# The preparation of an RWKV-7 layer in one written TensorE order, its key norms with tokens on partitions

## The chip, the cores and the metric

One core of one Trainium2 chip runs the whole kernel: two decoder layers over 256 tokens of width 2048, all in float32. The metric is the device time of one execution in microseconds, as the median of the runs.

## The reference, cut to what matters

The change lies in the even layer, in what comes ahead of its recurrence (group A) and of its window attention (group B):

```python
h = x @ e_w_in                                  # 256 x 2048 times 2048 x 4640
# A: 16 heads of 64; r, k, v of 1024 columns each, then low ranks of 64, 64 and 160
h = h + (token_shift(h) - h) * mu
w = -softplus(-(w0 + tanh(lw) @ w_up)) - 0.5;  decay = exp(-exp(w))
a = sigmoid(a0 + la @ a_up);  g = sigmoid(lg) @ g_up
kk = heads(k * k_k);  kk = kk / max(sqrt(sum(kk * kk, -1)), 1e-12)
k = k * (1 + (a - 1) * k_a)
# a scan over the tokens, for each head a state S of 64 x 64
S = S * decay + (S @ -kk) (kk * a)^T + v k^T;   y = S @ r
y = (y - mean(y)) * rsqrt(var(y) + 64e-5) * gn_w + gn_b + sum(r * k * r_k) * v
ya = y * g
# B: q of 1024, k and v of 128 columns: rotary, softmax over 128 tokens with sinks
mix = concat(ya, yb) @ e_w_out
```

After it come a layer norm, a SwiGLU, a second norm and a gated embedding, then the odd layer with the same.

## The kernel before, in words

**Products.** A float32 matrix is split into a rounded part `hi` and a rest `lo`, and a product is three TensorE products, `hi` by `xh`, `lo` by `xh`, `hi` by `xl`. Weights come in pieces of 2 x 128 rows: SyncE loads `raw`, ScalarE (ACT) casts `hi` (L151), VectorE (DVE) subtracts `lo` (L152); `hi` and `lo` have three buffers each, `raw` four. `gemm_steps` (L178 to L180) makes tokens by 512 columns in 96 products of 512 columns; `gemm_t` (L201, L203, L205) makes features by tokens, 192 products of 256 columns for 512 features. Small float32 products stand between them.

**The even layer's preparation**, `wkv_operands`, follows one path for two halves of 512 features (c = 0, 1):
- `incoming` loads x; for each of eight pairs j of 128 columns TensorE turns x (L216, four transposes), and ACT and DVE split it into `xh` and `xl` (L222, L223). The first `gemm_t` makes the low ranks out of it, 18 products for each j.
- From the low ranks come decays and gates (L586, L590, L591) and rates `a` (L625).
- `gemm_t` for k; the squares of kk are summed over a head's 64 features with the selector `sel` as weights (L633: 8 x 256 out), and the inverse norm is made on 8 partitions (two reciprocals and a square root with one Newton step). `gemm_t` for r.
- For each 128 features f: the norm is spread back (L651), decays are cumulated (L660), and DVE and ACT make the operands `ar` and `bk`. For each two f: the 32 x 32 blocks of the system to be solved (L689), copied into `blk` (L693).
- `values(0)` makes v for 512 columns, its token shift by DMA (`vs`, L719 to L721) and a copy with the head's mean removed (L723 to L725).
- The inverse of all 32 x 32 blocks, on DVE: a masked copy (L730), a transpose (L732), 30 steps of two operations (L739, L741), two transposes (L745, L746) into `Tc` and `TTc`.

Then `swa_project` makes keys (256 columns) and the first 512 columns of queries of group B, with rotary and transposes (L928, L945).

**The recurrence**, `wkv_chunks`, runs in units of 4 heads and 128 tokens. A unit makes masked matrices `lmat` (products L789, copies L790), solves with `Tc`, `TTc` (from L800 on) and ends in a tail on DVE (L880 to L891). `weave` runs two units at a time with products from a side: `values(1)` beside the first two units, the second 512 columns of queries beside the next two, the output projection and attention beside the rest.

**What sets the order.** In `wkv_operands` and for the first part of `swa_project` a scheduler orders every engine's instructions. From the first `weave` on TensorE's order is the written one. Each engine works its queue from the front: an instruction that waits holds up what stands behind it.

Of the kernel before, what the change touches and what calls it, by code (L numbers as in the profile page):

```python
# [18 lines left out]
P = 128  # L19
# [61 lines left out]

def take(steps, n):

    for _ in range(n):
        if next(steps, 0) == 0:
            return
        yield


class Trunk:  # L90
# [16 lines left out]
    def psum(self, mm, sm, sx=0):  # L107

        ctx = ExitStack()
        pool = lambda n, b: ctx.enter_context(self.tc.tile_pool(name=n, bufs=b, space=PSUM, reuse_waits="tile"))  # L110
        self.mm, self.sm = pool("mm", mm), pool("sm", sm)
        self.sx = pool("sx", sx) if sx else self.sm
        return ctx
# [70 lines left out]
    def gemm_t(self, lhs, view, n0, widths):  # L184
# [7 lines left out]
        for j, (xh, xl) in enumerate(lhs):  # L192
            hi, lo = next(ws)
            for kk in range(2):
                k = 2 * j + kk
                f0 = 0
                for i, w in enumerate(widths):
# [8 lines left out]
                                     skip_group_check=True)  # L206
        return [acc[i // 2][:w, i % 2] for i, w in enumerate(widths)]
# [203 lines left out]
def even_layer(T, a, src):  # L411
# [4 lines left out]
    with ExitStack() as ctx:  # L416
        ev = ctx.enter_context(tc.tile_pool(name="ev", bufs=1, reuse_waits="tile"))
        with tc.tile_pool(name="prep", bufs=1) as pr, T.psum(4, 4):
            ops, xT, values = wkv_operands(T, src, w_in, a, ev, pr)
            y = ops[-2]  # L420
        with tc.tile_pool(name="pairs", bufs=2, reuse_waits="tile") as pp, T.psum(2, 4, 2):
# [6 lines left out]
            swa = swa_project(T, pp, xT, w_in, a)  # L428
            qkv = next(swa)
            while next(swa) is None:  # L430
                pass
# [26 lines left out]
            with tc.manual_schedule(engines={mybir.EngineType.PE}):  # L458
                side = values(1, pp)
# [11 lines left out]
                side = zip_links(turned(), attend(range(4)), 2)  # L471
# [18 lines left out]
def wkv_operands(T, src, w_in, a, ev, pr):  # L490
    tc, nc = T.tc, T.nc
    xT = []
# [24 lines left out]
    nc.sync.dma_start(out=vec[50:51, 0:32], in_=mu[3328:3360].rearrange("(n p) -> n p", p=32))  # L517
    vps = T.sm.tile([P, 64], F32, name="s")
# [11 lines left out]
    early = tc.tile_pool(name="early", bufs=1)  # L530
    er = early.__enter__()
    gup0 = er.tile([P, AW], F32, name="gup0")
    gup1 = er.tile([32, AW], F32, name="gup1")
    nc.sync.dma_start(out=gup0, in_=a["e_g_up"][0][0:128])
    nc.sync.dma_start(out=gup1, in_=a["e_g_up"][0][128:160])
# [23 lines left out]
    for i in range(2):  # L559
        nc.vector.tensor_tensor(out=cum[:, i], in0=cum[:, i], in1=half, op=ALU.subtract)  # L560
# [8 lines left out]
    lg0 = er.tile([P, SEQ], F32, name="lg0")  # L569
    lg1 = er.tile([32, SEQ], F32, name="lg1")  # L570
    mix(ps[0], P, MU_L, lm)
    mix(ps[1], P, MU_L + 1, lg0)
    mix(ps[2], 32, MU_L + 2, lg1)
    nc.scalar.activation(out=lm[0:64], in_=lm[0:64], func=AF.Tanh)
    nc.scalar.activation(out=lg0, in_=lg0, func=AF.Sigmoid)
    nc.scalar.activation(out=lg1, in_=lg1, func=AF.Sigmoid)
# [3 lines left out]
    for c in range(2):  # L580
        cs = slice(c * 512, (c + 1) * 512)
        w0 = T.row(a["e_w0"][0], c * 512, 512, "brow", pr, 2)
        for t in range(NT):
            ts = slice(t * P, (t + 1) * P)
            z = T.sm.tile([P, 512], F32, name="s")
            nc.tensor.matmul(z, lm[0:64, ts], ups[0:64, cs], start=True, stop=True)  # L586
            nc.vector.tensor_tensor(out=sig[t][:, cs], in0=z, in1=w0, op=ALU.add)
            nc.scalar.activation(out=sig[t][:, cs], in_=sig[t][:, cs], func=AF.Sigmoid)
            g = T.sm.tile([P, 512], F32, name="s")
            nc.tensor.matmul(g, lg0[:, ts], gup0[:, cs], start=True, stop=False)  # L590
            nc.tensor.matmul(g, lg1[:, ts], gup1[:, cs], start=False, stop=True)  # L591
            nc.scalar.copy(out=gate[t][:, cs], in_=g)
    early.__exit__(None, None, None)
    T.rotary_tables(a["positions"][0])


    late = tc.tile_pool(name="late", bufs=1, reuse_waits="tile")
    lt = late.__enter__()
# [6 lines left out]
    for b in range(4):  # L605
        nc.vector.tensor_copy(out=m32[32 * b:32 * b + 32], in_=mtri[32 * b:32 * b + 32, 32 * b:32 * b + 32])
# [6 lines left out]
    ft = lambda n: lt.tile([P, SEQ], F32, name=n, bufs=4)  # L613
    bs = [ev.tile([P, AH], F32, name=f"bs{t}") for t in range(NT)]
    for c in range(2):
        k, kk, av, rks = [], [], [], []
        ps = T.gemm_t(xT, w_in, AW + c * 512, [128] * 4)
        for i in range(4):
            k.append(ft("k"))
            mix(ps[i], P, MU_K + 4 * c + i, k[i])  # L620
        ss = T.sm.tile([8, SEQ], F32, name="s")
        for i in range(4):
# [3 lines left out]
            av.append(ft("a"))  # L626
            nc.scalar.activation(out=av[i], in_=pa, func=AF.Sigmoid, bias=col[:, A0 + f:A0 + f + 1])
            kk.append(ft("kk"))
            nc.vector.tensor_scalar(out=kk[i], in0=k[i], scalar1=col[:, KK + f:KK + f + 1], scalar2=None,
                                    op0=ALU.mult)  # L630
            sq = lt.tile([P, SEQ], F32, name="sq")
            nc.scalar.activation(out=sq, in_=kk[i], func=AF.Square)
# [611 lines left out]
```

## Time and profile before

| | us |
|---|---|
| median of 3 runs | 2597.84 (2597.6 to 2606.3) |
| profiled execution | 2597.83 |
| its span, first to last instruction | 2595.9 |
| TensorE (PE) busy | 2541.7 (98%) |
| VectorE (DVE) busy | 1478.8 (57%) |
| ScalarE (ACT) busy | 1140.3 (44%) |
| even layer up to the end of the recurrence | about 475 |

Times in rows are microseconds from the span's start. A matmul's recorded time is longer than its share of the engine, since products overlap: the start of one to the start of the next is what it costs. Idle time stands in square brackets with what ended it.

### The profile page before, as it was taken

The numbers are of one execution on the slowest core, as the hardware profiler recorded it, in microseconds if no ns is written. First come the engines' busy times: TensorE is split into PE (matmuls) and PEld (weight loads), VectorE is DVE, ScalarE is ACT, GpSimd is POOL, SyncE is SP. The second block draws the span as 40 slices with busy tenths as digits, with TensorE's granted clock in tenths as the row PEclk, the third lists the DMA queues.
The fourth block names the chain that finished last, engine by engine and source line by source line (L and its number), as shares of the span: only waits on it lengthen the run. The fifth ranks groups of instructions, "written<-read, shape, count | busy, mean of one in ns | idle before, by whom it ended". The sixth has DMA issues, their size and how long they took to land.

```text
span 2595.9 us, 32573 instructions
## 1 busy us (share of the span) xinstructions
PE 2541.7 (98%) x12509; PEld 2083.3 (80%) x12509; DVE 1478.8 (57%) x2144; ACT 1140.3 (44%) x1508; POOL 60.3 (2%) x126
## 2 busy tenths in 40 slices
PE   8999989999999999999999999999999999999999
PEld 6887766778888888888888888887888888888877
DVE  4668556774544454455756666657454444445574
ACT  5563344444444344443444444435444334444343
POOL 0002110000000000000000000000000000000000
PEclk9999989999999999999999999999999999999999
DMA  6445322666666666666666555557666666666654
GB/s 190 129 119 170 106 66 74 199 208 190 187 190 191 194 197 187 189 189 192 201 193 193 170 171 168 165 171 220 193 187 188 193 194 194 187 189 188 193 179 159
DMA packets 240858, 458.56 MB, mean 177 GB/s; under 512 B 15345, under 2 KB 21155, under 8 KB 240703
## 3 DMA queue, kind: packets, MB, share of 16 engines
q1 hardware_dynamic: 240702, 456.48, 58.2%
q8 instruction: 98, 1.61, 0.2%
q14 instruction: 58, 0.47, 0.1%
HBM read 453.28 MB, written 2.10 MB: 175 GB/s over the span
## 4 chain that ended last, share of the span: by engine, by line
PE 90%; DVE 5%; ACT 1%; DMA 1%; issue 1%; POOL 0%; SPq 0%; DVEq 0%; ACTq 0%; POOLq 0%
PE acc L178 27%; PE acc L180 26%; PE acc L179 26%; PE acc L201 1%; PE acc L205 1%; PE acc L203 1%; DVE lo L152 1%; PE s L216 1%; DVE lmat L790 1%; ACT hi L151 0%; PE s L806 0%; PE s L1090 0%; PE s L1118 0%; DMA lnb<-in_ln_b_dram 0%; DMA raw<-in_e_w_in_dram 0%
## 5 line engine op out<-in xcount | busy, mean ns | idle before, releaser
L152 DVE TENSOR_TENSOR lo<-raw,hi 128x1024 fp32r<-128x1024 f32 (+1 forms) x840 | 1018.4, 1214 | 936.9 <-ACT hi L151 935.7
L151 ACT CAST hi<-raw 128x1024 fp32r<-128x1024 f32 (+1 forms) x840 | 875.3, 1043 | 1196.5 <-PE acc L180 1073.6
L178 PE MATMUL acc<-hi,x0h 128*128 128x512 f32 (+1 forms) x292 | 119.8, 410 | 1.8 <-ACT x L923 0.8
L180 PE MATMUL acc<-hi,x0l 128*128 128x512 f32 (+1 forms) x292 | 117.3, 402 | 0.0
L178 PE MATMUL acc<-hi,x1h 128*128 128x512 f32 (+1 forms) x292 | 116.6, 399 | 0.0
L179 PE MATMUL acc<-lo,x5h 128*128 128x512 f32 (+1 forms) x292 | 113.5, 389 | 2.1 <-DVE lo L152 2.1
L178 PE MATMUL acc<-hi,x6h 128*128 128x512 f32 (+1 forms) x292 | 114.4, 393 | 1.2 <-DVE x L288 1.2
L178 PE MATMUL acc<-hi,x2h 128*128 128x512 f32 (+1 forms) x292 | 115.5, 396 | 0.0
L178 PE MATMUL acc<-hi,x4h 128*128 128x512 f32 (+1 forms) x292 | 115.5, 396 | 0.0
L179 PE MATMUL acc<-lo,x0h 128*128 128x512 f32 (+1 forms) x292 | 115.4, 395 | 0.0
L178 PE MATMUL acc<-hi,x5h 128*128 128x512 f32 (+1 forms) x292 | 115.3, 395 | 0.0
L179 PE MATMUL acc<-lo,x3h 128*128 128x512 f32 (+1 forms) x292 | 113.7, 389 | 1.4 <-DVE lo L152 1.3
L178 PE MATMUL acc<-hi,x3h 128*128 128x512 f32 (+1 forms) x292 | 115.0, 394 | 0.0
L179 PE MATMUL acc<-lo,x4h 128*128 128x512 f32 (+1 forms) x292 | 113.6, 389 | 1.4 <-DVE lo L152 1.4
L179 PE MATMUL acc<-lo,x6h 128*128 128x512 f32 (+1 forms) x292 | 113.5, 389 | 1.4 <-DVE lo L152 1.4
L180 PE MATMUL acc<-hi,x1l 128*128 128x512 f32 (+1 forms) x292 | 114.6, 393 | 0.0
L179 PE MATMUL acc<-lo,x2h 128*128 128x512 f32 (+1 forms) x292 | 113.9, 390 | 0.4 <-DVE lo L152 0.4
L178 PE MATMUL acc<-hi,x7h 128*128 128x512 f32 (+1 forms) x292 | 114.0, 391 | 0.0
L179 PE MATMUL acc<-lo,x1h 128*128 128x512 f32 (+1 forms) x292 | 113.9, 390 | 0.0
L180 PE MATMUL acc<-hi,x2l 128*128 128x512 f32 (+1 forms) x292 | 113.9, 390 | 0.0
L180 PE MATMUL acc<-hi,x3l 128*128 128x512 f32 (+1 forms) x292 | 113.7, 390 | 0.0
L180 PE MATMUL acc<-hi,x4l 128*128 128x512 f32 (+1 forms) x292 | 113.5, 389 | 0.0
(571 smaller groups left out, 5082.3 us busy)
## 6 DMA issues: line engine op xcount, KB each, us to landing
raw<-in_ffn_w_dram SPq DMA_DIRECT2D x528, 512.0 KB, 3.6
raw<-in_o_w_in_dram SPq DMA_DIRECT2D x96, 512.0 KB, 3.8
raw<-in_e_w_in_dram SPq DMA_DIRECT2D x64, 512.0 KB, 3.7
raw<-in_ple_w_gate_dram SPq DMA_DIRECT2D x64, 512.0 KB, 4.8
raw<-in_e_w_out_dram SPq DMA_DIRECT2D x32, 512.0 KB, 4.9
raw<-in_o_w_out_dram SPq DMA_DIRECT2D x32, 512.0 KB, 4.0
x<-in_x_dram SPq DMA_DIRECT2D x16, 256.0 KB, 4.4
lng<-in_ln_g_dram SPq DMA_DIRECT2D x16, 256.0 KB, 3.3
```

The lines of the kernel that those rows point to most:

```text
L151: nc.scalar.copy(out=hi, in_=raw)
L152: nc.vector.tensor_tensor(out=lo, in0=raw, in1=hi.bitcast(F32), op=ALU.subtract)
L178: nc.tensor.matmul(o, xh[:, kk, s], hi[:, kk], start=k == 0, stop=False)
L179: nc.tensor.matmul(o, xh[:, kk, s], lo[:, kk], start=False, stop=False)
L180: nc.tensor.matmul(o, xl[:, kk, s], hi[:, kk], start=False, stop=k == 2 * n - 1)
L201: nc.tensor.matmul(o, hi[:, kk, fs], xh[:, kk], start=k == 0 and i % 2 == 0, stop=False, skip_group_check=True)
L203: nc.tensor.matmul(o, lo[:, kk, fs], xh[:, kk], start=False, stop=False, skip_group_check=True)
L205: nc.tensor.matmul(o, hi[:, kk, fs], xl[:, kk], start=False, stop=k == nk - 1, skip_group_check=True)
L216: nc.tensor.transpose(ps[:, kk, t * P:(t + 1) * P], src[t][:, kk * P:(kk + 1) * P], self.ident)
L790: nc.vector.copy_predicated(lm4[:, i].rearrange("p a b -> p (a b)"), mask, pl.rearrange("p a b c -> p (a b c)"))
```

## The change

`wkv_operands` gets a written order. For its first part (x, the low ranks) PE, ACT and DVE all keep the order in which the program issues, and `incoming` turns one j ahead of the product; from then on TensorE alone does. The small products are cut into steps, and `through` lets one step follow each step of a projection (12 products of 256 columns, or 6 of 512): decays and gates in the k projection of half 0, squares in r's, operands of half 0 in k's and r's of half 1, operands of half 1 in `values(0)` and the first queries, whose projection now stands ahead of the keys'. The inverse is issued beside the queries and keys. Transposes of queries and keys wait in a list `late` and are put at counted places of a later projection.

The norms' sums have tokens on partitions: the squares are the weights and `sel` with 8 columns is streamed (L686), one power on GpSimd makes the inverse norm, two transposes bring it back. The separate copy of v without its mean goes; the mean is taken from y (three DVE operations on `py` where ACT had a copy). Half of `cum` and the mask `m32` are made on GpSimd.

```diff
+def trailing(steps, late, at):
+    n = 0
+    while True:
+        try:
+            next(steps)
+        except StopIteration as e:
+            return e.value
+        yield
+        n += 1
+        if late and n in at:
+            late.pop(0)()
...
-        for j in range(8):
-            if j % 2 == 0:
+        for j in range(9):
+            if j < 8 and j % 2 == 0:
...
-            xT.append(T.split_t([x[t][:, j * 256:(j + 1) * 256] for t in range(NT)], f"x{j}", T.xt))
-            yield xT[-1]
-    ps = T.gemm_t(incoming(), w_in, 3 * AW, [128, 128, 32])
+            if j < 8:
+                xT.append(T.split_t([x[t][:, j * 256:(j + 1) * 256] for t in range(NT)], f"x{j}", T.xt))
+            if j:
+                yield xT[j - 1]
+    first = T.gemm_t_steps(incoming(), w_in, 3 * AW, [128, 128, 32])
+    manual = tc.manual_schedule(engines={E.PE, E.Activation, E.DVE})
+    manual.__enter__()
+    last(take(first, 10))
...
-            nc.tensor.matmul(ss, sel[:, i], sq, start=i == 0, stop=i == 3)
...
+                nc.tensor.matmul(ss[:, t], sq[i][:, t * P:(t + 1) * P], sel[:, i], start=i == 0 and t == 0,
+                                 stop=i == 3, skip_group_check=True)
+            yield
+        n = lt.tile([P, NT, 8], F32, name="norm")
+        nf = n.rearrange("p t h -> p (t h)")
+        nc.vector.tensor_scalar(out=n, in0=ss, scalar1=1e-24, scalar2=None, op0=ALU.max)
+        nc.gpsimd.tensor_tensor(out=nf, in0=nf, in1=T.mhalf, op=ALU.pow)
...
+        at = {0: (feature, 0), 4: (feature, 1), 9: (feature, 2), 11: (blocks, 2 * c, 0), 12: (blocks, 2 * c, 1),
+              13: (feature, 3), 20: (blocks, 2 * c + 1, 0), 21: (blocks, 2 * c + 1, 1), 22: (bonus, 0), 23: (bonus, 1)}
...
-            vm = pool.tile([P, 8], F32, name=f"vm{t}", bufs=1)
-            nc.vector.tensor_reduce(out=vm, in_=v3[t][:, h], axis=AX.X, op=ALU.add)
-            nc.vector.tensor_scalar(out=vm, in0=vm, scalar1=1.0 / HD, scalar2=None, op0=ALU.mult)
-            nc.vector.tensor_tensor(out=vs3[t][:, h], in0=v3[t][:, h],
-                                    in1=vm[:, :, None].to_broadcast([P, 8, HD]), op=ALU.subtract)
...
+    through(products(("k", 0), AW), side)
+    last(side)
+    with tc.tile_pool(name="late", bufs=1, reuse_waits="tile") as lt:
...
+        last(rates(0, lt))
+        through(products(("r", 0), 0), ks[0])
+        last(ks[0])
+        through(products(("k", 1), AW + 512), os[0])
+        through(products(("r", 1), 512), os[0], ks[1])
+        last(os[0])
+        last(ks[1])
+        through(values(0, pr), os[1])
+        swa = keys_, queries, late, qkv = swa_project(T, xT, w_in, a)
+        through(queries(0, pr), os[1], inv, inv)
+        through(trailing(keys_(), late, (9, 12)), os[1], inv)
+        last(inv)
...
-            nc.scalar.copy(out=y, in_=py)
+            nc.vector.tensor_reduce(out=var, in_=py, axis=AX.X, op=ALU.add)
+            nc.vector.tensor_scalar(out=var, in0=var, scalar1=1.0 / HD, scalar2=None, op0=ALU.mult)
+            nc.vector.tensor_tensor(out=y, in0=py, in1=var[:, :, None].to_broadcast([P, G, HD]), op=ALU.subtract)
...
-                side = swa
+                side = queries(1, pp)
...
-                side = zip_links(turned(), attend(range(4)), 2)
+                side = zip_links(trailing(turned(), late, (4, 7)), attend(range(4)), 2)
```

What stands in a row is shown at three places. **ACT at the start**, where `hi` is a cast of a weight piece and `x0h`, `x1h` and so on are casts of a turned j. Before:

```order
L151 CAST hi<-raw 128x576 x3
L222 CAST x0h<-s 128x512
L222 CAST x1h<-s 128x512
L151 CAST hi<-raw 128x576 x2
L222 CAST x2h<-s 128x512
L222 CAST x3h<-s 128x512
L222 CAST x4h<-s 128x512
L151 CAST hi<-raw 128x576 x3
```

ACT in the changed kernel, from its first cast:

```order
L237 CAST x0h<-s 128x512
L237 CAST x1h<-s 128x512
L165 CAST hi<-raw 128x576
L237 CAST x2h<-s 128x512
L165 CAST hi<-raw 128x576
L237 CAST x3h<-s 128x512
L165 CAST hi<-raw 128x576
```

The casts went from groups to turns: each `hi` but the first now stands behind the cast of the next j, and on TensorE the transposes of that j stand behind the 18 products of the j before last.

**DVE where the inverse begins**, whose first operation is the masked copy into `blk`. Before:

```order
L676 TENSOR_TENSOR kk<-r,k 128x256
L152 TENSOR_TENSOR lo<-raw,hi 128x1024
L698 COPY bs_539<-s 128x8
L698 COPY bs_540<-s 128x8
L152 TENSOR_TENSOR lo<-raw,hi 128x1024
L730 COPY_PREDICATED blk_536<-m_531,blk_538 128x1024
```

DVE in the changed kernel at the same operation (L798 there):

```order
L790 TENSOR_TENSOR vs_2057<-vs_2057,brow 128x512
L789 TENSOR_TENSOR vs_2058<-vs_2058,v_507 128x512
L791 TENSOR_TENSOR v_506<-vs_2057,v_506 128x512
L790 TENSOR_TENSOR vs_2058<-vs_2058,brow 128x512
L166 TENSOR_TENSOR lo<-raw,hi 128x1024
L791 TENSOR_TENSOR v_507<-vs_2058,v_507 128x512
L166 TENSOR_TENSOR lo<-raw,hi 128x1024
L798 COPY_PREDICATED blk_501<-m_496,blk_503 128x1024
```

The whole of `values(0)` moved ahead of the inverse: on TensorE the last blocks (L750 there) now stand after 132 products of 512 columns of v and queries, where 25 stood ahead of them.

**TensorE ahead of the first solve product**, which reads the inverse `blk` and `lmat`. Before:

```order
L789 MATMUL s<-ar_1176,bk_1177 128x256 x2
L945 MATMUL sx<-ident,q 128x128 x4
L789 MATMUL s<-ar_1176,bk_1177 128x256 x2
L789 MATMUL s<-ar_1203,bk_1204 128x256
L945 MATMUL sx<-ident,q 128x128 x4
L789 MATMUL s<-ar_1203,bk_1204 128x256 x3
L178 MATMUL acc<-hi,x0h 128x512
L800 MATMUL s<-blk_538,lmat_2226 32x32 x8
```

TensorE in the changed kernel at the same place:

```order
L883 MATMUL s<-ar_1316,bk_1317 128x256 x4
L883 MATMUL s<-ar_1419,bk_1420 128x256 x4
L192 MATMUL acc<-hi,x0h 128x512
L193 MATMUL acc<-lo,x0h 128x512
L194 MATMUL acc<-hi,x0l 128x512
L894 MATMUL s<-blk_503,lmat_2565 32x32 x8
L900 MATMUL s<-v_506,lmat_2565 128x64 x4
```

The transposes of the queries left this place, and six more products of `values(1)` stand ahead of the solve; 60 products of the queries and the 96 of the keys now stand between the last blocks and these rows, where 167 of v and queries and the 96 stood.

## Rows read from the trace of the kernel before

**Rows 1.** Busy us (count) of PE, PEld, DVE, ACT, POOL; granted clock, DMA share, GB/s.
```profile
10.65:33.30 22.65, 22.26 (x168) 20.49 (x169) 14.41 (x43) 10.34 (x16) 1.35 (x5) 1.00 0.75 245
...
51.06:182.40 131.34, 128.70 (x931) 113.07 (x930) 80.58 (x142) 75.05 (x129) 0.53 (x1) 0.99 0.43 125
182.40:250.74 68.34, 62.30 (x326) 50.53 (x324) 63.55 (x142) 27.99 (x42) 13.98 (x15) 1.00 0.59 173
...
285.86:340.34 54.48, 46.74 (x330) 36.40 (x329) 33.44 (x72) 15.19 (x23) 8.74 (x13) 0.92 0.33 97
```
**Rows 2.** ACT in order of time, at the start: start, duration, instruction, idle before.
```profile
9.44 0.67 ACT L151 CAST hi<-raw 128x576 fp32r<-128x576 f32 x1 [2.13 <-DMA raw<-in_e_w_in_dram]
10.02 0.58 ACT L222 CAST x0h<-s 128x512 fp32r<-128x512 f32 x1
...
19.07 0.59 ACT L222 CAST x4h<-s 128x512 fp32r<-128x512 f32 x1 [0.45 <-PE s L216]
```
**Rows 3.** DVE and PE in order of time, at the start.
```profile
10.14 0.76 DVE L152 TENSOR_TENSOR lo<-raw,hi 128x576 fp32r<-128x576 f32 x1 [2.04 <-ACT hi L151]
...
10.65 0.58 PE L201 MATMUL acc<-x0h,hi 128*128 128x256 f32 x1 [4.43 <-ACT x0h L222]
...
13.21 0.41 PE L201 MATMUL acc<-x0h,hi 128*128 128x256 f32 x1
...
13.42 0.42 PE L203 MATMUL acc<-x0h,lo 128*128 128x256 f32 x1
...
18.76 0.60 PE L216 MATMUL s<-ident,x 128*128 128x128 f32 x4
```
**Rows 4.** PE around one small product (L625) in a projection.
```profile
69.75 0.28 PE L205 MATMUL acc<-x7l,hi 128*128 128x256 f32 x1
69.96 0.70 PE L625 MATMUL s<-lm,ups 64*128 64x256 f32 x2
70.58 0.39 PE L201 MATMUL acc<-x0h,hi 128*128 128x256 f32 x1
70.81 0.28 PE L203 MATMUL acc<-x0h,lo 128*128 128x256 f32 x1
```
**Rows 5.** Groups on DVE from 185.7 to 235: busy, mean ns, idle before.
```profile
L152 DVE TENSOR_TENSOR lo<-raw,hi 128x1024 fp32r<-128x1024 f32 x9 | 10.9, 1215 | 0.7 <-ACT hi L151 0.7
...
L725 DVE TENSOR_TENSOR vs<-v,vm 128x512 f32<-128x512 f32 x2 | 1.4, 686 | 0.0
```
**Rows 6.** DVE in order of time: the inverse's ends, then the first masked copies.
```profile
185.77 1.36 DVE L730 COPY_PREDICATED blk<-m,blk 128x1024 f32<-128x1024 uint8 x1 [1.43 <-ACT blk L693]
...
232.87 1.20 DVE L746 STREAM_TRANSPOSE blk<-blk 128x1024 f32<-128x1024 f32 x1
...
238.86 2.59 DVE L790 COPY_PREDICATED lmat<-mask,s 128x512 f32<-128x512 uint8 x4
```
**Rows 7.** GpSimd in order of time, behind the inverse.
```profile
234.21 5.45 POOL L795 COPY TT<-blk 32x128 f32<-32x128 f32 x4 [21.24 <-DVE blk L746]
239.72 1.81 POOL L766 MEMSET lmat<- 128x2048 f32 x1
241.59 3.57 POOL L795 COPY TT<-blk 32x128 f32<-32x128 f32 x4
```
**Rows 8.** PE's waits from 285.86 to 345: in total, times, longest.
```profile
PE sx L945 <- DVE q L401: 4.5, 1, 4.5
PE s L800 <- DVE lmat L790: 2.1, 1, 2.1
```
**Rows 9.** Busy time by shorter stretches, columns as in rows 1.
```profile
55.00:65.00 10.00, 10.00 (x86) 10.00 (x85) 3.77 (x4) 3.83 (x4) 0.00 (x0) 1.00 0.58 162
...
338.00:345.00 7.00, 5.68 (x28) 5.04 (x30) 4.83 (x11) 0.59 (x1) 0.00 (x0) 0.52 0.57 148
...
182.90:197.50 14.60, 14.60 (x65) 12.06 (x66) 12.57 (x26) 8.11 (x14) 0.00 (x0) 1.00 0.40 109
...
205.00:214.00 9.00, 6.15 (x48) 5.34 (x47) 8.97 (x21) 1.36 (x3) 3.45 (x6) 1.00 0.42 117
```

More of the change, by code (lines that the diff above doesn't have):

```diff
@@ L426, in turn @@
                 ya[j] = T.split_t([y[t][:, j * 256:(j + 1) * 256] for t in range(NT)], f"x{j}", T.xt, ps)
[L428 to L431, printed above, removed]
+            _, queries, late, qkv = swa
             attend = lambda fs: swa_attend(T, pp, fs, yb, *qkv)
@@ L517, in wkv_operands @@
     nc.sync.dma_start(out=vec[50:51, 0:32], in_=mu[3328:3360].rearrange("(n p) -> n p", p=32))
+    ps = last(first)
     vps = T.sm.tile([P, 64], F32, name="s")
@@ L612, in wkv_operands, with until, rates @@
     c2 = lambda u: u.rearrange("p (c t) -> p c t", t=P)
-    ft = lambda n: lt.tile([P, SEQ], F32, name=n, bufs=4)
     bs = [ev.tile([P, AH], F32, name=f"bs{t}") for t in range(NT)]
[L615 to L621, printed above, removed]
+    done, made = {}, {}
+    def until(name):
+        while name not in done:
+            yield
+    def rates(c, lt):
+        av = made["a", c] = []
         for i in range(4):
@@ L650, in wkv_operands, with operands, feature @@
+    def operands(c, lt):
+        yield from until(("inv", c))
+        yield from until(("r", c))
+        ps, k, av, inv = done["r", c], made["k", c], made["a", c], made["inv", c]
+        r = [lt.tile([P, SEQ], F32, name="r", bufs=4) for i in range(4)]
+        mix(ps[0], P, MU_R + 4 * c, r[0])
+        def feature(i):
+            f = 4 * c + i
             pi = T.sm.tile([P, SEQ], F32, name="s")
             nc.tensor.matmul(pi, selT[:, i], inv, start=True, stop=True)
+            pc = T.sm.tile([P, NT, 2, P], F32, name="s")
+            for t in range(NT):
+                nc.tensor.matmul(pc[:, t], sig[t][:, f * P:(f + 1) * P], cum, start=True, stop=True)
@@ L694, in wkv_operands, with blocks @@
-        for t in range(NT):
+        def blocks(g, par):
+            s = slice(64 * par, 64 * par + 64)
+            pl = T.sm.tile([P, 2, NT, P], F32, name="s")
+            for fi in range(2):
+                for t in range(NT):
+                    nc.tensor.matmul(pl[:, fi, t], BK[2 * g + fi][s, t, 0], AR[2 * g + fi][s, t, 0],
+                                     start=True, stop=True)
+            for b in range(4):
+                q = slice(32 * b, 32 * b + 32)
+                nc.scalar.copy(out=bview[q, g, par], in_=pl[q, :, :, q])
@@ L707, in values @@
     def values(c, pool):
         acc = yield from T.gemm_steps(xT, w_in, 2 * AW + c * 512)
[L710 to L711 removed]
+        cs = slice(c * 512, (c + 1) * 512)
+        muv = T.row(mu, 2 * AW + c * 512, 512, "brow", pool, 1)
+        vs = [ev.tile([P, 512], F32, name=f"vs{t}") for t in range(NT)]
+        nc.gpsimd.memset(vs[0][0:1], 0.0)
         for t in range(NT):
@@ new lines, in products, with through @@
+    def products(name, n0):
+        done[name] = yield from T.gemm_t_steps(xT, w_in, n0, [128] * 4)
+    def through(main, *sides):
+        for _ in main:
+            for side in sides:
+                next(side, None)
+    through(products(("k", 0), AW), side)
+    last(side)
+    with tc.tile_pool(name="late", bufs=1, reuse_waits="tile") as lt:
+        ks = [keys(0, lt), keys(1, lt)]
+        os = [operands(0, lt), operands(1, lt)]
+        inv = inverse(lt)
+        last(rates(0, lt))
[10 more added lines that the diff above has]
+        last(inv)
```

302 lines of the change are left out of this document (156 added, 146 removed).

## Prediction

> **What bounds the kernel now.** The page comes first: TensorE (PE) is busy 98% of the span and the chain that ended last is 90% PE. So only three things can move the time: PE's waits, its granted clock, and what its own products cost. The instructions behind the recurrence are the same in both kernels, so I cut the trace into stretches up to there [rows 1]. From 10.65 to 33.3, the low ranks, PE is busy 22.26 of 22.65 us. From 51.06 to 182.4, the two k and r projections with their small products, it waits 2.6 us. From 182.4 to 250.74, between the last 32 x 32 blocks and the first product of the solve, it waits 6.0 us, and DVE is the loaded engine: busy 63.55 of 68.34 us. From 285.86 to 340.34 PE waits 7.7 us at a clock of 0.92. A perfect order of the preparation could thus win some 10 us and the 4.4 us that PE waits ahead of its first real product [rows 3]. That is little against 2597, so what the written order adds matters as much as what it takes away.
>
> **The start: low ranks.** Before, ACT cast three weight pieces, the third only when its load had landed, and then `x0h` at 10.02 [rows 2]; PE began at 10.65, though its transposes were over 4.43 us earlier, at 6.22 [rows 3]. Now `x0h` and `x1h` come first on ACT. With `x1h` behind transposes that end by 6.22 at the latest, then one cast and one subtraction, PE starts about 3 us sooner.
>
> Behind that the order costs. In the changed kernel each `hi` stands on ACT behind the cast of the next j; that cast waits for the transposes of that j, and these stand on PE behind the 18 products of the step. So nothing of a step's weights is ready when its products could begin. One round, by rows: four transposes 0.60 [rows 3]; the cast of `xh` 0.49 (0.58 long, but 10.02 lies 0.09 ahead of the end of the cast before it) and of `hi` 0.67 [rows 2]; `lo` 0.76, 0.03 behind `hi` [rows 3]; two handovers of 0.05 (10.60 to 10.65); then the 17 products that need `lo`, at 0.12 each (86 in 10 us [rows 9]), 2.04. That is 4.7 us. A dense round is 18 x 0.12 and four transposes at about 0.1: 2.55. PE loses 2.15 in each of six rounds (the first is counted in the start, and behind the last transposes two pieces follow each other): 12.9. Less the 3 us, and less about 0.8 for PE's waits in this stretch and the one transpose of the vectors that now stands behind it: **+9**. Bounds: +6 if casts and subtraction overlap more than the rows show, +12 if the earlier start brings nothing because the clock then rises later.
>
> **Counted places.** In the changed order of PE, 43 small groups stand inside projections up to the last blocks where some 27 stood. A switch costs 0.09 going in (69.75 to 69.96 in place of 0.12) and 0.11 coming back (70.58 to 70.81) [rows 4]: 16 x 0.2 = 3.2. The 2.6 us of waits go [rows 1]: between a product and the one that needs its result now lie four or five steps of 12 products, 5.8 us and more, and no cast or DVE operation in these rows is longer than 1.2. If that cover fails somewhere the old waits are back. **+0.6**.
>
> **The norms and the mean.** Eight products with 256 columns become sixteen with 8 columns, and four small transposes come in. At 0.62 for a small product [rows 4] the old eight cost at most 5 us; the new twenty are short but each loads its weights. I take 0, bounds -2 and +2. The power on GpSimd has no row with 16 columns; five steps of the r projection (7 us) hide it, and copies there took 1.4 us each at the slowest [rows 7]. The ACT and DVE operations that go are worth nothing where PE is the bound.
>
> **The inverse.** It starts when ACT has copied the last blocks, and PE's solve waits for it. Before, 185.77 to 234.07: 48.3 us [rows 6], DVE never idle for long. In the changed queue five wide `lo` stand inside it where nine stood: 4 x 1.2 less [rows 5]. The shift and the mean of v, ten operations of 512 columns at 0.6 to 0.69 [rows 5], are ahead of it or gone: 6.4 less. Twelve rotary operations of the queries come in; I count 0.2 each, as they are small against the 0.69 of 512 columns: 2.4 more. Their projection ends while the chain runs, so some waiting comes in as well, about 0.5. That gives 40 (37 to 43). Ahead of it lie 2.5 us of copies (3.4 before, for eight; four now stand behind the last blocks). Behind it nothing covers any more: the first solve product needs a PSUM buffer that is free only when `lmat` of the second unit is copied, which needs its memset, which stands on GpSimd behind four copies: 5.45 + 1.81 + 0.65 + 0.1 = 8 [rows 6, 7]. With the faster copies (3.57) it is 6.1. Sum from the last blocks to the solve: 50.5.
>
> Before, this took 68.34. But 107 products of 512 columns now stand ahead of the last blocks, at 0.225 (65 in 14.6 us [rows 9]) 24.1 us, and six of `values(1)` more stand ahead of the solve, 1.4. The same work before, in the same place: 68.3 - 24.1 + 1.4 = 45.6. So **+5**: the work that hid the inverse was moved ahead of it. PE will wait some 11 us in one piece where it waited 6 in several. Bounds: 0 and +8.
>
> For the GpSimd copies, rows 7 show four in 5.45 us while DVE ran its memset and masked copies, and four in 3.57 later. The Trainium skill (SBUF — State Buffer, section "SBUF: two separate sides", on the port pair that Vector and GpSimd share) says that the two exclude each other for whole instructions. By that rule the copies stay slow here, as DVE has the same operations behind the inverse: with 5.45 the term is the +5, with 3.57 it would be +3.
>
> **Later.** The wait of 4.5 us ahead of the queries' transposes [rows 8] goes, as they move into the next weave. But DVE worked off the units' tails in that time, and the next units' products need PSUM buffers that the same tails and masked copies free: of the 4.5 I let 1.5 be won (0 to 6, with clock). Each tail gets longer by two reductions' worth, and `values(1)` loses the mean's operations: 0 (-2 to +2; 2.1 us of wait stands there now [rows 8]). A long wait lowers the clock: behind the 4.5 us it was 0.52 for 7 us [rows 9]. After 11 us of waiting I count **+2** (0 to 3.4, seven us at half pace with PE the bound). Together **+0.5**.
>
> **Sum.** 9 + 0.6 + 0 + 5 + 0.5 = +15 on the profiled 2597.83, whose median of three is 2597.84: **2613 us**.
>
> **Rivals.**
> *The clock stays low at the start.* Products stood 0.21 apart (13.21 to 13.42 [rows 3]) before the clock had risen, 0.12 later: 1.2 and 2.4 GHz. With 2.1 us idle in each round it may not rise until the rounds are over. Then each round gets 17 x 0.09 and some 0.4 for its transposes more, 1.9, in six rounds 11: **2624**. For it: it fell behind 4.5 us of waiting [rows 9]. Against it: from 205 to 214 PE was busy 6.15 of 9 us and the clock stayed at 1.00 [rows 9]. The Trainium skill (TensorE: Matmul & The Clock Gate, section "What's actually happening") has the low rate as the default, which activity lifts; by that rule a start in short bursts may stay slow and the time is the 2624 of this rival. Chance 0.15.
>
> *The later waits were worth more.* If unit products find free buffers, the 4.5 us go whole, the 7 us at 0.52 give back 3.4, and the 2.1 us of the `lmat` wait go too: -10. With the start at +6, the inverse at 0 and the places at +0.6 that is **2594**, not slower. It decides at the first products of the third pair of units: do they start before DVE is through with the tails? The queue has the tails and the copies mixed, so I doubt it. Chance 0.12.
>
> *The written order changes less than it says.* PE's waits around the inverse may only change their place, since DVE was the bound there before as well; then that term is 0, the start alone remains, and with the later 1.5 and without a clock loss it is 2597.8 + 9 + 0.6 - 1.5 = **2606**. Chance 0.25.
>
> **How the numbers follow.** My forecast has 0.48, spread from 2606 to 2620, about two thirds of it slower by more than 0.5% (2610.8), which is about what a measurement of this kernel can tell from no change. With the first rival and a little of the third: slower 0.52. Faster by over 0.5% (under 2584.9) is only a part of the second rival: 0.05. Same: 0.43. The range holds the forecast, most of the first and of the third rival: 2600 to 2627.
>
> **What would show it.** At the start: six gaps of about 2 us on PE, each ended by DVE's `lo`, and the first 144 products ending near 42 in place of 33.3. Between the last blocks and the solve: a gap of about 10 us ended by the `lmat` copies, with DVE busy throughout, and a low clock behind it. Between 60 and 200 hardly a wait. At the third pair of units: no wait at the queries' transposes, but one at the units' own products or at attention's. The forecast is wrong if ACT's casts run ahead of TensorE at the start, or if the inverse ends while the keys' products still run.

## The result and the profile after

The changed kernel takes 2624.1 us (median of four, 2620.8 to 2626.3), the kernel before 2601.99 in the same comparison (2597.6 to 2606.3): 1.0084 times as long, interval 1.0058 to 1.0110. The profiled execution of the changed kernel took 2620.79 us, 22.96 more than the profiled 2597.83 of before. The recurrence ends 23.0 us later, and nothing is won or lost behind it. So the stages, cut at the starts of the same instructions of both traces, hold the whole difference:

| us from the span's start | before | after | difference of the stage |
|---|---|---|---|
| first real product | 10.65 | 7.95 | -2.7 |
| last of the 144 low-rank products | 33.4 | 49.5 | +18.8 |
| last product of the four k and r projections | 163.4 | 178.2 | -1.4 |
| first product of the solve | 250.7 | 270.8 | +5.3 |
| second pair of units | 285.9 | 306.3 | +0.4 |
| fourth pair of units | 408.7 | 433.9 | +4.8 |
| end of the recurrence | 474.8 | 497.9 | -2.1 |

The stretches of the changed kernel that answer to [rows 1]; busy us (count) of PE, PEld, DVE, ACT, POOL, then granted clock, DMA share, GB/s:

```profile
7.95:49.72 41.77, 31.44 (x168) 26.49 (x169) 12.15 (x18) 9.51 (x15) 1.89 (x6) 0.84 0.58 166
49.72:178.32 128.60, 128.60 (x919) 113.03 (x918) 64.30 (x116) 72.91 (x116) 6.77 (x2) 1.00 0.47 136
178.32:220.28 41.96, 41.96 (x190) 32.11 (x189) 30.32 (x57) 26.15 (x46) 0.97 (x2) 1.00 0.55 153
220.28:270.79 50.51, 38.88 (x226) 33.45 (x225) 45.06 (x117) 15.66 (x27) 7.24 (x15) 0.86 0.47 129
270.79:306.26 35.47, 35.47 (x306) 27.61 (x305) 16.80 (x35) 13.81 (x25) 6.39 (x9) 1.00 0.32 90
306.26:359.58 53.32, 48.54 (x321) 37.77 (x321) 27.03 (x54) 13.85 (x20) 8.08 (x12) 0.87 0.33 100
```

Read the first number behind the length: PE is busy without a gap from 49.72 to 220.28, which is what the counted places were to give. The gaps are in the first stretch (10.3 us), ahead of the solve (11.6) and in the second pair of units (4.8), and in just these three the granted clock is below 1 (1.00 stands for 2.4 GHz, 0.50 for 1.2). The column doesn't show the slow beginning: the first products stand 0.21 apart in both kernels, from 13.21 to 13.42 in [rows 3] and from 11.92 to 12.13 here, and it still says 1.00 for that time.

The start, PE, ACT and DVE in order of time (start, duration, instruction, idle before); they answer to [rows 2, 3]:

```profile
13.65 0.59 ACT L237 CAST x2h<-s 128x512 fp32r<-128x512 f32 x1 [5.76 <-PE s L231]
14.13 0.67 ACT L165 CAST hi<-raw 128x576 fp32r<-128x576 f32 x1
14.86 0.39 PE L215 MATMUL acc<-x1h,hi 128*128 128x256 f32 x1 [1.25 <-ACT hi L165]
14.88 0.75 DVE L166 TENSOR_TENSOR lo<-raw,hi 128x576 fp32r<-128x576 f32 x1
15.68 0.39 PE L217 MATMUL acc<-x1h,lo 128*128 128x256 f32 x1 [0.43 <-DVE lo L166]
...
17.80 0.60 PE L231 MATMUL s<-ident,x 128*128 128x128 f32 x4
...
20.93 0.28 PE L217 MATMUL acc<-x2h,lo 128*128 128x256 f32 x1
21.05 0.33 PE L219 MATMUL acc<-x2l,hi 128*128 128x256 f32 x1
21.17 0.42 PE L215 MATMUL acc<-x2h,hi 128*32 128x256 f32 x1
21.38 0.42 PE L217 MATMUL acc<-x2h,lo 128*32 128x256 f32 x1
```

One round is the chain of the prediction, link by link: ACT waits 5.76 us for the transposes, casts `x2h`, only then `hi`; PE waits 1.25 for `hi`, makes one product, and waits 0.43 more for `lo`. But see the last rows too: within a row of products the step from one to the next goes from 0.12 to 0.21. The clock falls while PE is busy; this round and the one before it had 1.7 us of idle time each. By rounds, columns as above:

```profile
17.80:23.73 5.93, 4.25 (x24) 3.59 (x23) 1.36 (x2) 1.16 (x2) 0.00 (x0) 0.78 0.71 167
...
29.67:34.89 5.22, 3.54 (x23) 2.89 (x23) 1.49 (x3) 1.16 (x2) 0.00 (x0) 0.84 0.19 35
```

A round was to take 4.7 us; from the second on it takes 5.2 to 5.9 at a clock of 0.78 to 0.84.

The inverse on DVE, and GpSimd behind it; they answer to [rows 6, 7]:

```profile
222.04 1.33 DVE L798 COPY_PREDICATED blk<-m,blk 128x1024 f32<-128x1024 uint8 x1 [0.41 <-ACT blk L754]
...
259.42 1.21 DVE L813 STREAM_TRANSPOSE blk<-blk 128x1024 f32<-128x1024 f32 x1
260.54 0.39 DVE L857 CAST mask<-lmat 128x512 uint8<-128x512 f32 x1
261.31 1.76 DVE L860 MEMSET lmat<- 128x2048 f32 x1 [0.38 <-issue]
263.18 2.54 DVE L884 COPY_PREDICATED lmat<-mask,s 128x512 f32<-128x512 uint8 x4
266.14 1.33 DVE L884 COPY_PREDICATED lmat<-mask,s 128x512 f32<-128x512 uint8 x2 [0.41 <-POOL TT L889]
```
```profile
260.77 1.70 POOL L889 COPY TT<-blk 32x128 f32<-32x128 f32 x4 [14.21 <-DVE blk L813]
262.53 1.80 POOL L860 MEMSET lmat<- 128x2048 f32 x1
264.40 1.74 POOL L889 COPY TT<-blk 32x128 f32<-32x128 f32 x4
```

The inverse takes 38.6 us (222.04 to 260.63; 48.3 in [rows 6]) and the first solve product follows 10.2 us behind it, at 270.79. PE's waits from the end of the projections to the solve:

```profile
PE s L883 <- DVE lmat L884: 9.4, 1, 9.4
PE acc L193 <- DVE lo L166: 2.2, 1, 2.2
```

The wait ends at 263.96, with DVE's first masked copy; ahead of that copy stand the mask (260.54) and DVE's own memset (261.31). Behind the wait the clock is down: PE's next 6.9 us were granted 0.54.

```profile
263.90:270.80 6.90, 6.84 (x24) 5.25 (x24) 4.49 (x8) 0.00 (x0) 2.01 (x5) 0.54 0.33 34
```

### The profile page after: what moved, and what is told of

It reads as the page before. It is cut to its first block, busy times and chain, and to the rows that moved or that the text cites. A ratio compares the mean times of both kernels' runs of the same rounds, so it can differ in the third digit from the quotient of the medians.

```text
span 2619.1 us, 32597 instructions
## 1 busy us (share of the span) xinstructions
PE 2557.5 (98%) x12529; PEld 2099.2 (80%) x12529; DVE 1467.0 (56%) x2133; ACT 1135.1 (43%) x1496; POOL 62.5 (2%) x136
## 4 chain that ended last, share of the span: by engine, by line
PE 83%; DVE 3%; DMA 1%; issue 0%; ACT 0%; POOL 0%; DVEq 0%; SPq 0%; ACTq 0%; POOLq 0%
PE acc L192 26%; PE acc L194 26%; PE acc L193 26%; PE s L231 1%; DVE lo L166 1%; PE s L1191 0%; PE s L1219 0%; DVE lmat L884 0%; DMA lnb<-in_ln_b_dram 0%; DVE x L284 0%; PE s L900 0%; PE s L290 0%; DMA raw<-in_ffn_w_dram 0%; PE sx L1096 0%; PE sx L1090 0%
## 5 line engine op out<-in xcount | busy, mean ns | idle before, releaser
L166 DVE TENSOR_TENSOR lo<-raw,hi 128x1024 fp32r<-128x1024 f32 (+2 forms) x840 | 1018.7, 1214 | 933.5 <-ACT hi L165 932.0
L165 ACT CAST hi<-raw 128x1024 fp32r<-128x1024 f32 (+2 forms) x840 | 877.0, 1045 | 1198.8 <-PE acc L194 1065.0
L194 PE MATMUL acc<-hi,x6l 128*128 128x512 f32 (+1 forms) x292 | 113.5, 389 | 0.0
L194 PE MATMUL acc<-hi,x5l 128*128 128x512 f32 (+1 forms) x292 | 113.4, 388 | 0.0
```

The costliest lines, as they stand in the source:

```text
L165: nc.scalar.copy(out=hi, in_=raw)
L166: nc.vector.tensor_tensor(out=lo, in0=raw, in1=hi.bitcast(F32), op=ALU.subtract)
L194: nc.tensor.matmul(o, xl[:, kk, s], hi[:, kk], start=False, stop=k == 2 * n - 1)
```

## The experiments

### The start: order of the casts

**e1.** Weights first. In `gemm_t_steps`:

```diff
-        for j, (xh, xl) in enumerate(lhs):
-            hi, lo = next(ws)
+        turns = iter(lhs)
+        for j in range(nk // 2):
+            if j:
+                hi, lo = next(ws)
+                xh, xl = next(turns)
+            else:
+                xh, xl = next(turns)
+                hi, lo = next(ws)
```

> The changed kernel, with one thing altered: from the second step of the low ranks on, a step's weight piece is cast ahead of the next turn's cast, so hi stands on ACT (and lo on DVE) ahead of work that waits for the next transposes. Theory of the serial chain: the six pairs of waits (1.25 us for hi, 0.43 for lo) go, TensorE is dense again and its clock rises, the 144 products end at 30 to 34 us in place of 49.7, and the whole is 15 to 19 us shorter (ratio to the kernel before about 1.002). Rival, the low clock alone (the early start is what keeps it low, the waits only fill idle time): products stay at 0.21 us, the stage ends at 43 to 46, the whole is 4 to 7 us shorter.

Measured: 2599.99 us against 2599.19 for the kernel before, ratio 1.0000 (0.9991 to 1.0009); the 144 products end at 30.2 us in place of 49.5. One stretch of e1, and its waits up to 31 us:

```profile
7.53:30.45 22.92, 22.69 (x169) 21.52 (x169) 10.88 (x17) 9.47 (x15) 2.66 (x8) 1.00 0.90 270
```
```profile
PE acc L221 <- ACT hi L165: 1.2, 1, 1.2
PE acc L223 <- DVE lo L166: 0.2, 1, 0.2
```

In the changed kernel the same waits were these:

```profile
PE acc L215 <- ACT hi L165: 8.7, 7, 1.2
PE acc L217 <- DVE lo L166: 2.9, 7, 0.4
```

Only the first `hi` is still waited for. PE does 18 products and four transposes in 2.55 us, the dense round of the prediction. The early start then pays as well: 3 us ahead of the kernel before. By the profiled spans e1 lies 20.4 us below the changed kernel (2598.7 and 2619.1), a little more than expected.

**e2.** Fillers. In `incoming`, behind the transposes of turns 2 to 7:

```diff
+            if 1 < j < 8:
+                pad = T.sm.tile([P, SEQ], F32, name="s")
+                for i in range(6):
+                    nc.tensor.matmul(pad, xT[0][0][:, 0, 0:P], xT[0][0][:, 0], start=True, stop=True)
```

> The changed kernel with six products of 256 columns that nobody reads behind the transposes of each turn from the third on, in the time in which TensorE waits for hi. The chain of ACT and DVE is as it was. If the lower clock in the rounds comes from the idle time and costs on its own: the 17 products of every round take 2.05 us (0.12 each) and a round 5.0 to 5.2, so the stage ends at 43 to 45 in place of 49.7. If the clock is low there for another reason, the rounds stay at 5.2 to 5.9 or get longer by the six products, 0.7 to 1.3 each, and the stage ends at 50 to 56.

Measured (one run): 2617.57; 144 products by 43.4 us, 6.1 earlier, though PE has 36 products more to do (0.95 us a round); a round takes 4.79 us, and behind the slow beginning the stage is granted the full clock:

```profile
7.66:43.65 35.99, 30.44 (x205) 26.82 (x205) 11.86 (x18) 9.51 (x15) 2.10 (x7) 1.00 0.60 181
```

The chain is unchanged, and PE's first round in the changed kernel, at 1.00, takes these 4.79 us too, if its slow transposes (1.05 in place of 0.60) are allowed for: only the clock differs. So the chain alone costs 10.0 us (43.4 against 33.4, with the earlier start in it) and the lower clock 6.1 on top.

**e10.** TensorE's order alone:

```diff
-    manual = tc.manual_schedule(engines={E.PE, E.Activation, E.DVE})
+    manual = tc.manual_schedule(engines={E.PE})
```

> The changed kernel with TensorE alone in the written order in the first part, too; ACT and DVE are ordered by the scheduler there, which puts three hi ahead of x0h and stays two pieces ahead. If the written order of ACT and DVE is what costs: as e1, the first part ends at 29 to 34 us in place of 49.7 and the whole takes 2599 to 2605. If TensorE's written order (turns one ahead) costs itself: 40 or later, 2610 or more.

Measured (one run): 2600.44, the 144 products by 32.4, though PE begins at 10.93, so that the earlier start is gone as well. TensorE's written order, with turns one ahead, costs nothing; ACT's and DVE's does.

**e12.** The mirror image: in the kernel before, `incoming` turns one ahead, and around the first product

```diff
+    E = mybir.EngineType
+    with tc.manual_schedule(engines={E.PE, E.Activation, E.DVE}):
+        ps = T.gemm_t(incoming(), w_in, 3 * AW, [128, 128, 32])
```

> The kernel before, with one part of the change alone: turns one ahead of the products and TensorE, ACT and DVE in the order of issue for the low ranks; all else is as before. By the theory of the serial chain the first 144 products end at 48 to 51 us in place of 33.3 and the whole is 14 to 18 us longer than 2599. If the chain costs only together with what follows it in the changed kernel: 5 us or less.

Measured (one run): 2613.81, 14.5 above the 2599.27 of before on that chip; the 144 products end at 50.6. This part alone makes most of the change's loss of 22.

### The inverse

**e3.** Operands twice as fast:

```diff
-        through(values(0, pr), os[1])
+        through(values(0, pr), os[1], os[1])
```

> The changed kernel with the operands of half 1 at two steps for each step of values(0) in place of one, so that the last 32 x 32 blocks stand ahead of nearly all products of the queries. Nothing else is altered. Theory of the moved cover: the inverse starts 11 to 13 us earlier (209 in place of 222), runs as long (38 to 40), and PE's waits of 2.2 and 9.4 us ahead of the solve go or nearly so; the first solve product comes 8 to 11 us earlier than 270.8, and the whole is 8 to 11 us shorter. Rival, DVE is the bound of the whole stretch and PE's waits only change place: waits come in among the operands (2 us and more) and the first solve moves by 3 us or less.

Measured: 2617.26, ratio to the kernel before 1.0065 (1.0048 to 1.0082). The inverse starts at 206.12 but takes 45.3, and the solve comes at 266.80. Once the 0.9 by which this run's first part was shorter are taken off, the inverse starts 15.0 us earlier and the solve 3.1. DVE in order of time, and PE's waits up to the solve:

```profile
206.12 1.35 DVE L798 COPY_PREDICATED blk<-m,blk 128x1024 f32<-128x1024 uint8 x1 [3.23 <-ACT blk L754]
...
250.23 1.22 DVE L813 STREAM_TRANSPOSE blk<-blk 128x1024 f32<-128x1024 f32 x1
251.36 0.39 DVE L857 CAST mask<-lmat 128x512 uint8<-128x512 f32 x1
252.13 1.76 DVE L860 MEMSET lmat<- 128x2048 f32 x1 [0.38 <-issue]
```
```profile
PE acc L193 <- DVE lo L166: 8.3, 2, 5.0
```

The 9.4 us for `lmat` are gone and 8.3 for `lo` have come: the pieces of later products now stand on DVE among the inverse and behind the copies of `lmat`. My expectation of 8 to 11 was wrong, and the rival's account is the nearer one: the waits change place. But they come at the keys' products (3.3 us) and at the first of `values(1)` (5.0), not among the operands, as it says, and the 3.1 lies at its bound of 3.

**e4.** The preparation of `lmat` on GpSimd:

```diff
-    nc.vector.tensor_copy(out=mask, in_=lmats[1][:, 0].rearrange("p a b -> p (a b)"))
+    nc.gpsimd.tensor_copy(out=mask, in_=lmats[1][:, 0].rearrange("p a b -> p (a b)"))
...
-        (nc.gpsimd if i else nc.vector).memset(lmats[i], 0.0)
+        nc.gpsimd.memset(lmats[i], 0.0)
```

> The changed kernel with the cast of mask and both large memsets of lmat on GpSimd, where they stand ahead of the copies out of the inverse and run while it does. If what stands behind the inverse on DVE and GpSimd is on the path (mask 0.39, memset 1.76 with its 0.4 of waiting, memset 1.8 ahead of the copies for lmat1): from the inverse's last transpose to the first solve product 5.5 to 6.5 us in place of 10.2, so the whole is about 4 us shorter. If the eight masked copies and the PSUM buffers set that time alone, 9 us or more stay and the whole moves by less than 1.5.

Measured (one run): 2618.17; from the inverse's end to the solve 7.1 us in place of 10.2; the recurrence ends 3.0 earlier. On the path, then, if a little less than expected.

**e9.** Half of the inverse:

```diff
-        for k in range(1, 31):
+        for k in range(1, 16):
```

> The changed kernel with 15 of the 30 steps of the inverse left out, so that what is computed is no longer the inverse; the order of everything else is as it was. In the changed kernel those steps stand on DVE from 240 to 257.6 and take some 10 us of its time. If DVE's work between the last blocks and the solve is what the solve waits for: the first solve product comes 8 to 11 us earlier than 270.8. If TensorE's own products and the masked copies behind the inverse set it, as moving the blocks alone (e3) might suggest: 4 us or less.

Measured (one run): 2612.82; the inverse takes 21.3 us, 17.3 less, and the solve comes at 264.23, 6.3 earlier with the start's 0.2 taken off: between the two expectations. What has come in its place:

```profile
PE acc L193 <- DVE lo L166: 4.9, 1, 4.9
```

DVE's queue holds the inverse's two transposes (3.0 us) ahead of the keys' `lo`. Of 17.3 us taken off DVE's chain PE gets 6.3.

### Tails and turns

**e5.** The mean back in `values`. The three operations on `py` in the tail become the ACT copy of before, and in `values` (with `vs` of full width, and read by the products):

```diff
+            nc.vector.tensor_reduce(out=vm, in_=v3[t][:, h], axis=AX.X, op=ALU.add)
+            nc.vector.tensor_scalar(out=vm, in0=vm, scalar1=1.0 / HD, scalar2=None, op0=ALU.mult)
+            nc.vector.tensor_tensor(out=vs3[t][:, h], in0=v3[t][:, h],
+                                    in1=vm[:, :, None].to_broadcast([P, 8, HD]), op=ALU.subtract)
```

> The changed kernel with the mean of v removed as in the kernel before: a separate copy vs made in values(), products that read vs, and in the tail of a unit the ACT copy in place of the three DVE operations on py. Theory of the longer tail: in the second pair of units the masked copies of lmat stand on DVE behind the tails of the first pair, so the first solve product comes 10.5 to 12.5 us behind the pair's first product in place of 16.8 (10.3 before the change); the stretch from the second pair to the third takes 48 to 50 us in place of 53.3 and the whole is 3 to 5 us shorter. Rival, the lower clock behind the long wait at the inverse sets that stretch: it stays within 1 us of 53.3.

Measured: 2615.58 us, ratio to the kernel before 1.0062 (1.0044 to 1.0081), 8.5 below the changed kernel by the medians and 4.7 by the spans of the profiled executions (2614.4 and 2619.1). The intervals of the two ratios overlap (the changed kernel's begins at 1.0058), so the stages have to show what the edit does. First DVE in the second pair of units of the changed kernel:

```profile
299.51 0.42 DVE L972 TENSOR_REDUCE var<-s 128x4 f32<-128x256 f32 x1 [2.88 <-PE s L967]
299.97 0.17 DVE L973 TENSOR_SCALAR var<-var 128x4 f32<-128x4 f32 x1
300.17 0.42 DVE L974 TENSOR_TENSOR y<-s,var 128x256 f32<-128x256 f32 x1
...
314.07 0.42 DVE L987 TENSOR_TENSOR v<-y,gate 128x256 f32<-128x256 f32 x1
...
315.01 0.72 DVE L884 COPY_PREDICATED lmat<-mask,s 128x512 f32<-128x512 uint8 x1
```

PE's products of that pair begin at 306.26; the two tails end on DVE at 314.5, and all but one of the masked copies stand behind them. The solve comes 16.8 us behind the pair's first product. PE's waits in this pair, in the changed kernel:

```profile
PE s L883 <- DVE lmat L884: 4.8, 1, 4.8
```

And in e5:

```profile
PE s L902 <- DVE lmat L892: 2.1, 1, 2.1
PE s L908 <- DVE lmat L892: 1.2, 1, 1.2
```

In e5 the distance is 10.3 (308.78 to 319.09) and the pair's stretch 48.5 in place of 53.3. It is 16.7 to 16.8 in e1, e3, e6 and e11 too, which leave the mean in the tail, and 10.3 in the kernel before, e7 and e8, which don't. From the second to the fourth pair it takes 119.4 us; the changed kernel 127.6, the kernel before 122.9. Its price stands earlier: the solve is 3.0 later than in the changed kernel, measured from the projections' end, as the six operations on `vm` and `vs` are back on DVE.

**e6.** Transposes of the second queries put back ahead of the third pair:

```diff
                 last(side)
+                late.pop(0)()
+                late.pop(0)()
```

> The changed kernel with the transposes of the second half of the queries put back to where they stood, ahead of the third pair of units. If moving them won time: PE waits there for the rotary on DVE, 3 to 5 us, the stretch from the second pair's first product to the fourth's grows from 127.6 us by 1.5 to 4. If the wait is only handed to the masked copies that follow (2.8 and 0.7 us now): it stays within 1 us.

Measured (one run): 2626.39. PE waits for the rotary there as it did in [rows 8], and longer:

```profile
PE sx L1047 <- DVE q L416: 6.7, 1, 6.7
```

From the second to the fourth pair it is 129.0 us, 1.4 more: between the two expectations, and by a single run. The move is worth little: with the turns back the waits of these pairs add up to 5.0 us more (the rotary's come, those for `lmat` in the third pair go), while PE's products take 3.6 less (busy 110.0 in place of 113.6).

### Together

**e7** is e1, e4 and e5 in one kernel; **e8** has e3 as well; **e11** is e8 without e5.

> The changed kernel with three edits together: weight pieces cast ahead of the next turn (as in e1), mask and memsets on GpSimd (as in e4), the mean removed from v as before (as in e5). If the terms add: 21 less for the start against the changed kernel, 3 for the masks, 3 to 5 for the tail: 2592 to 2597 where the kernel before has 2599 (ratio 0.997 to 0.9995). If each only moves a wait of DVE further down: no less than e1, 2599 to 2601.

> As e7, and the operands of half 1 at two steps for each step of values(0) (as in e3). If DVE's queue between the last blocks and the solve is the bound, the solve comes about 3 us earlier again: 2589 to 2594. If with the masks gone the waits for lo (3.3 and 5.0 us in e3) go as well, the solve comes 6 to 9 earlier: 2585 to 2590. If the waits only change place it is the time of e7 within 1 us.

> As e8 (start, masks, operands twice), but the mean is taken from y, as in the changed kernel. If the mean's place is worth what e5 showed: the first solve product comes 2 to 3 us earlier than in e8 (247.5) and the second pair of units takes 3 to 5 us longer (47.4 there), so the whole lies 1 to 4 us above e8, 2588 to 2591. If the tails have become free in the new order: below e8, 2584 to 2587.

| | median us | ratio to before, interval | 144 products by | solve | second pair | fourth pair | recurrence ends |
|---|---|---|---|---|---|---|---|
| before | 2599.2 to 2602.0 | | 33.4 | 250.7 | 285.9 | 408.7 | 474.8 |
| e1 | 2599.99 | 1.0000, 0.9991 to 1.0009 | 30.2 | 251.3 | 286.8 | 412.4 | 476.4 |
| e7 | 2593.88 | 0.9976, 0.9967 to 0.9985 | 31.2 | 254.6 | 290.1 | 409.5 | 475.6 |
| e11 | 2595.65 | 0.9980, 0.9971 to 0.9990 | 30.2 | 247.7 | 283.4 | 408.7 | 472.7 |
| e8 | 2587.04 | 0.9953, 0.9939 to 0.9967 | 30.2 | 247.5 | 283.3 | 402.2 | 466.7 |

e8 beats both kernels: it is 0.5% below the kernel before, and 37 us below the changed kernel by the medians (34 by the ratios). Against e7 the solve is 7.1 earlier, 6.2 once the 1.0 is taken off by which its first part was shorter, where e3 alone gave 3.1: with mask and memsets off DVE, and the blocks early, the waits for `lo` and `lmat` are small as well:

```profile
PE acc L193 <- DVE lo L166: 4.2, 2, 2.8
PE s L897 <- DVE lmat L898: 1.7, 1, 1.7
```

The terms don't simply add, though: of the 3.0 that e4 gave ahead of the solve, e7 shows 1.0 against e5 (94.6 in place of 95.6 from the projections' last product to the solve).

e11 missed its expectation upward. The solve isn't earlier without the mean's operations (247.7), so nothing is gained ahead of it, and the second and third pairs cost the tail's price in full: 125.4 us against 118.9.

## Why the prediction was right or wrong

The time, 2624, lies in the range, and the side was right. By the point it was 15 us forecast and 22 to 23 measured; the terms:

**The start: right mechanism, too small by 7.** +9 forecast, +16.1 measured (33.4 to 49.5). The earlier start is there (2.7 of the 3), and the round of 4.7 us is e2's 4.79 to within 0.1. With the chain alone the stage ends at 43.4, and I had said "near 42". The step that failed stands one paragraph on: the clock falling in these rounds was put among the rivals with a chance of 0.15 and a price of 11. It did fall, not for all products but for part of them, and e2 prices it at 6.1. I let [rows 9] speak against it (6.15 busy of 9 us at 1.00); those were two gaps, of 0.75 and 2.1 us and six apart, here a gap of 1.7 came in every round. That this is the difference no run shows; e2 shows that with 1.0 in every round the clock stays. So the outcome is neither forecast nor rival, but the forecast plus half of the rival. That the median is this rival's 2624 to the microsecond is luck: by the rival the change costs 26 us, 20 of them at the start; it cost 22 to 23, 16.1 of them there, and the kernel before took 4 us more in this comparison than in the runs that the forecast starts from.

**Counted places, norms and mean: a little better than forecast.** +0.6 and 0 forecast, -1.4 measured, with no wait at all in 170 us. The cover that I named (four or five steps between a product and the one that needs its result) held everywhere. Whether the switches cost less than forecast or the norms' products won something isn't separated: by the traces one of the old sums of squares cost 0.53, two of the new ones 0.36, and neither part was tried alone.

**The inverse: right size, mechanism half right.** +5 forecast, +5.3 measured; 38.6 us for the inverse against 40, a gap of 9.4 us ended by the `lmat` copies, a clock of 0.54 behind it against 0.52 in [rows 9]. That the sum from the last blocks to the solve is met to the tenth (50.5 forecast, 220.28 to 270.79 measured) is luck: 1.8 in place of 2.5 ahead of the inverse, 38.6 in place of 40, and 10.2 in place of 8 behind it. But "the work that hid the inverse was moved ahead of it" says that an earlier inverse brings the time back, and e3 brought back 3.1 us of it for 15.0. DVE's queue is the other bound: the inverse, the `lo` of what should cover it and the masked copies pass through one engine. The rival "PE's waits only change their place" was wrong for the change itself, yet it is what happens when one tries to undo it by moving the blocks alone. And the path behind the inverse was wrong: I summed 8 us through slow GpSimd copies (5.45) and the memset behind them. The copies took 1.70, and PE waited for DVE's mask, its own memset, which I had left out, and the first masked copy: 3.3. The other 6.8 are PE's own products at the lower clock: the second half of the products for `lmat` took 4.3 us from 263.96 on, the first half 2.0 from 250.90 on, at 1.00. So about half of the 6.8 is the clock's price, which I had put under "Later" with 2.

**Later: +0.5 forecast, +3.0 measured.** The step that failed is "each tail gets longer by two reductions' worth, and `values(1)` loses the mean's operations: 0". Counted as work it is about 0. But the tail's operations stand ahead of the masked copies that PE waits for. e5 shows the place: 16.8 us to the second pair's solve against 10.3, 8.2 us over two pairs, with 3.0 of it paid earlier. The clock behind the long wait, 2 us of this term, fell ahead of the solve instead, so this step missed by more than the sum shows. In the better order the mean's new place costs all of its price (e11 against e8: 8.6 by the medians, 6.4 in the second and third pairs).

**Rivals.** "The later waits were worth more" fell at the point that I had named: the third pair of units waits for `lmat` on DVE (2.8 us), not for the rotary. Putting the turns back (e6, one run) cost 1.4 there.

## What to carry to other kernels

In an order written by hand, ask of every instruction what the one ahead of it waits for: a cast that needs only a load doesn't belong behind one that needs TensorE, and its place on ACT and DVE was worth 19 us here, while TensorE's own order cost nothing. Price a small operation by who waits behind it, not by its length: three operations of 0.2 to 0.4 us in a tail cost 6 to 8 us over two pairs of units. And when a wait is taken away on a loaded engine, look for the next in its queue before counting the gain; here single moves ahead of the solve gave 3 us of a 9 us wait, and four edits together gave back more than the whole loss.

## What the runs showed of the hardware

Two things that I had not expected. The clock can fall within a row of products, as at 21.17 us above, with the idle time ahead of the row and in the round before; 36 products that nobody reads, 0.95 us a round, kept it at 1.00 and won 6 us net.

The GpSimd copies of 32 x 128 out of the inverse take 0.39 us each in some places and several times that in others. Eight of them in e4, where DVE ran masked copies out of PSUM at the same time:

```profile
260.98 3.48 POOL L889 COPY TT<-blk 32x128 f32<-32x128 f32 x8 [12.88 <-DVE blk L813]
```
```profile
260.84 2.51 DVE L884 COPY_PREDICATED lmat<-mask,s 128x512 f32<-128x512 uint8 x4
```

In [rows 7] four took 5.45 us, when DVE in the kernel before ran these:

```profile
234.76 1.76 DVE L766 MEMSET lmat<- 128x2048 f32 x1 [0.38 <-issue]
236.44 2.49 DVE L152 TENSOR_TENSOR lo<-raw,hi 128x1024 fp32r<-128x1024 f32 x2
```

A memset stood beside the fast copies of the changed kernel too (261.31), so `lo`, which reads two operands from SBUF, is the likelier cause. The traces bear it out copy by copy. In the changed kernel, later:

```profile
282.07 1.95 POOL L889 COPY TT<-blk 32x128 f32<-32x128 f32 x2 [15.93 <-PE s L922]
282.51 1.23 DVE L166 TENSOR_TENSOR lo<-raw,hi 128x1024 fp32r<-128x1024 f32 x1 [1.71 <-ACT hi L165]
```

The first of the two copies takes 0.41 us; the second starts with `lo` and takes 1.50, to 0.27 behind the end of `lo`. All fourteen traces have 224 such copies up to 300 us. The 42 that started while a `lo` was running took 0.88 to 1.50 and ended 0.25 to 0.28 behind it; 179 others took 0.38 to 0.45, also the 25 that had started just ahead of a `lo`. Three of 2.4 to 3.2 us are left, one of them in the 5.45 of [rows 7]: they started with DVE's memset, which held up no other copy, and why it held these stays open. The Trainium skill (SBUF — State Buffer, section "SBUF: two separate sides") says that a Vector operation with two SBUF inputs holds the shared ports against a GpSimd operation that reads SBUF; these rows agree with that. I had cited the same section for slow copies, and read [rows 7] as copies beside memset and masked copies, without looking at which DVE operations had stood there and which would stand beside them in the changed kernel.
